# Four more pairs of adaLN vectors computed as rows on VectorE inside the SwiGLUs

## The chip, the cores and the metric

The kernel runs on one core of one Trainium2 chip. The metric is the device time of one execution in microseconds (us); all times here are in that unit unless a line says ns. The engines of the core are named as in the profile: PE is TensorE's matrix multiply and PEld its load of stationary operands, DVE is VectorE, ACT is ScalarE, POOL is GpSimd, SP is the engine that issues most of the transfers.

## What is computed

Two layers of a diffusion backbone: 256 latent and 256 context tokens of width 1024, in fp32. A layer is a SwiGLU, four token mixers that share one normed input, and a second SwiGLU. Before each of the three stands an RMS norm that is modulated by a shift and a scale, and behind each a gate; the nine vectors (three times shift, scale, gate) are the adaLN vectors, made from a conditioning vector, one set for the latent and one for the context tokens:

```python
mod  = (silu(c)     @ ada_w[l] + ada_b[l]).reshape(B, 1, N_ADA, D_MODEL)   # latent
modc = (silu(c_ctx) @ ada_w[l] + ada_b[l]).reshape(N_ADA, D_MODEL)         # context
sh1, sc1, g1, sh2, sc2, g2, sh3, sc3, g3 = [mod[:, :, i] for i in range(N_ADA)]
x = x + 0.5 * g1 * swiglu(modulate(rms_norm(x, norm_g[l, 0]), sh1, sc1), w_gate, w_up, w_down)
y, yc = token_mixers(modulate(rms_norm(x, norm_g[l, 1]), sh2, sc2), ...)
x = x + g2 * y
x = x + 0.5 * g3 * swiglu(modulate(rms_norm(x, norm_g[l, 2]), sh3, sc3), ...)
# the same for the context tokens; at the end rms_norm(x, final_g)

def rms_norm(x, g):      return x * rsqrt(mean(x * x) + RMS_EPS) * g
def modulate(x, shift, scale):  return x * (1.0 + scale) + shift
def swiglu(x, w_gate, w_up, w_down):
    return (silu(x @ w_gate) * (x @ w_up)) @ w_down     # inner width 2816 = 22 * 128
```

What the change touches is only how `mod` and `modc` are computed; a vector has 1024 values for each of the two conditionings.

## The kernel before

**Layout.** Activations lie with the channels on the partitions: `x[m]`, m = 0 to 7, is a tile of 128 channels by 512 tokens (256 in the last SwiGLU, which has only the latent tokens). Every product of the network is made in three parts from operands that are split into a high part `h` and a low part `l` (`mm3`: h by h, h by l, l by h). So each weight tile `wr` is cast by ScalarE into `wh` (L315) and VectorE makes `wl` as the difference (L316), in two halves of 512 columns. While the last SwiGLU of layer 0 runs, the weights of layer 1 that are called LOWS (36 parts) are split ahead: `low_part` loads 0.52 MB, splits it and stores 1.05 MB to DRAM.

**A SwiGLU** is `ffn`. It goes through three groups of inner tiles, GROUPS: 8, 8 and 6. In a group there is first an *up step* for each inner tile (products `gu` of gate and up, 48 in all, then tanh and the multiplications), then eight *down sums* m = 0 to 7 (products `dn`: 24 in a group of 8, 18 in a group of 6), each of which ends with a residual `resid` on VectorE (L660), which adds the gated sum to `x[m]`, one instruction for latent and one for context tokens. Behind every up step and every down sum `side` is called: it may emit one step of side work, so that this stands between the instructions of the SwiGLU.

**A norm** is `norm` with `stats`: ScalarE squares the eight `x` tiles (the first into `nacc`, L505, the others into `sq`, L508), GpSimd adds six of the squares to `nacc` (L510), TensorE sums over channels with a product by ones, first of `nacc`, then of the eighth square (both are called `st`), VectorE takes ten small steps for the inverse root (`rsqrt`, L366 to L376), TensorE transposes the result to all partitions (`B`, L356). Then, per tile, VectorE forms `xg` (L543), ScalarE adds the shift into `uh` (L545) and VectorE makes the low part `ul` (L546); the next `gu` or mixer products use `uh` and `ul`.

**adaLN vectors** are computed in nine pairs per layer, PAIRS; a pair is named by (layer, index), and the index of a gate's pair is 2 (first SwiGLU), 5 (mixer) and 8 (second SwiGLU). There are two ways:

- `ada(l, i)` on TensorE: eight loads `aw` of 0.52 MB, sixteen fp32 products `ada` (32 records in the profile), then a copy by ScalarE, four transposes `adaT` and a few small VectorE steps.
- `ada_rows(l, i)` on VectorE: eight steps, each with one load `aw` of 0.52 MB, two multiplications with a running sum, `aj` (L472, one for each conditioning, 128 by 1024), and an addition of the bias (L475). VPAIRS lists the pairs that go this way; the weights for them are laid out transposed on the host.

Rows are side work of `ffn`. Before, `side` emits one step of rows after each up step, and after a down sum only where no LOWS are left; it emits one `low_part` after every step of either kind while there are any. The SwiGLUs had as rows: first of layer 0 and first of layer 1 the pairs 3, 4, 6, 7; second of layer 0 the pairs (1,0) and (1,1), and the LOWS. The gates' pairs are done by `ada` at the borders: (0,5) and (1,5) behind the norm ahead of a mixer, (0,8) and (1,8) behind the norm ahead of the second SwiGLU, (1,2) between the layers' SwiGLUs.

**What sets the order.** The kernel is written in program order, and a scheduler fixes one static order for each engine from it, by priorities and from its own estimate of when operands and buffers are ready. Buffers rotate: 3 for a raw weight `wr`, 8 each for `wh` and `wl`, 6 for the small tiles (`sq`, `nacc`, `xg`, `aj` and others), 5 or 6 for `aw`. A load can start when the buffer's earlier user is done; loads are issued in order on SP's queue.

The borders, in order of time: 439 us, first SwiGLU of layer 0 to its mixer; 1150 us, that mixer to the second SwiGLU; 1526 us, second SwiGLU to the first of layer 1; 1896 us, that SwiGLU to the mixer of layer 1; 2349 us, that mixer to the last SwiGLU.

## Time and profile before

| | before |
|---|---|
| three runs, us | 2561.84, 2573.04, 2575.85 |
| median, us | 2573.04 |
| the profiled execution, us | 2568.95 |
| its span, first to last instruction, us | 2567.2 |
| PE busy | 2491.3 us, 97% |
| DVE busy | 1714.1 us, 67% |
| ACT busy | 1080.1 us, 42% |
| POOL busy | 146.9 us, 6% |
| transfers | 444.56 MB, mean 173 GB/s |
| granted TensorE clock, mean | 0.989 |
| share of PE in the chain that ended last | 53% |

The profile page is one execution, taken by the hardware profiler. A busy time is the union of an engine's instructions; the granted clock is 1.00 at 2.4 GHz and 0.50 at 1.2 GHz. In a timeline, rows of the same kind that follow each other are folded into one with xN, its time being the busy time of all of them. What stands in brackets is the idle time of the engine ahead of the row and the engine, tile and line that ended it. A product written `128*32 128x512` has a stationary operand of 128 by 32 and a moving one of 128 by 512.

### The profile page before, as it was taken

The numbers are of one execution on the slowest core, as the hardware profiler recorded it, in microseconds if no ns is written. First come the engines' busy times: TensorE is split into PE (matmuls) and PEld (weight loads), VectorE is DVE, ScalarE is ACT, GpSimd is POOL, SyncE is SP. The second block draws the span as 40 slices with busy tenths as digits, with TensorE's granted clock in tenths as the row PEclk, the third lists the DMA queues.
The fourth block names the chain that finished last, engine by engine and source line by source line (L and its number), as shares of the span: only waits on it lengthen the run. The fifth ranks groups of instructions, "written<-read, shape, count | busy, mean of one in ns | idle before, by whom it ended". The sixth has DMA issues, their size and how long they took to land.

```text
span 2567.2 us, 37223 instructions
## 1 busy us (share of the span) xinstructions
PE 2491.3 (97%) x13624; PEld 2055.4 (80%) x13624; DVE 1714.1 (67%) x3533; ACT 1080.1 (42%) x2127; POOL 146.9 (6%) x212
## 2 busy tenths in 40 slices
PE   7999999999999999999999999999999999899998
PEld 4778887898877767777888878888888778797998
DVE  5667767677556768747676557767457666676665
ACT  4433223433555564434444433232345653254554
POOL 0110001000000000010000010000010034300000
PEclk9999999999999999999999999999999999999999
DMA  7455546332413123238998944545244379755554
GB/s 256 168 196 196 173 145 205 119 116 90 141 56 125 62 74 111 93 116 286 325 333 320 326 146 148 181 136 194 85 166 167 105 212 269 217 177 206 181 181 124
DMA packets 163847, 444.56 MB, mean 173 GB/s; under 512 B 18698, under 2 KB 24268, under 8 KB 163664
## 3 DMA queue, kind: packets, MB, share of 16 engines
q1 hardware_dynamic: 142928, 404.42, 46.8%
q0 software_dynamic: 20736, 37.76, 5.3%
q8 instruction: 108, 1.77, 0.3%
q14 instruction: 75, 0.61, 0.1%
HBM read 383.91 MB, written 58.20 MB: 172 GB/s over the span
## 4 chain that ended last, share of the span: by engine, by line
PE 53%; DVE 3%; DMA 2%; issue 1%; ACT 1%; POOL 0%; DVEq 0%; POOLq 0%; ACTq 0%
PE gu L305 24%; PE dn L305 12%; PE gate L305 6%; PE wo L305 3%; PE tm L305 2%; PE ada L305 1%; PE dp L305 1%; PE br L305 1%; PE O L305 1%; PE S L305 1%; PE PT L356 1%; PE Og L305 0%; DVE wl L316 0%; DMA wh<-h_w_gate 0%; PE bk L305 0%
## 5 line engine op out<-in xcount | busy, mean ns | idle before, releaser
L315 ACT CAST wh<-wr 128x512 fp32r<-128x512 f32 (+1 forms) x854 | 517.1, 613 | 945.0 <-PE gu L305 335.0
L316 DVE TENSOR_TENSOR wl<-wr,wh 128x512 fp32r<-128x512 f32 (+1 forms) x854 | 572.6, 680 | 351.1 <-ACT wh L315 341.0
L305 PE MATMUL gu<-uh,wh 128*128 128x512 f32 (+1 forms) x1408 | 512.1, 366 | 3.6 <-ACT uh L545 2.8
L305 PE MATMUL gu<-ul,wh 128*128 128x512 f32 (+1 forms) x1408 | 512.1, 365 | 0.0
L305 PE MATMUL gu<-uh,wl 128*128 128x512 f32 (+1 forms) x1408 | 511.7, 364 | 0.1
L305 PE MATMUL dn<-hh,wh 128*128 128x512 f32 (+1 forms) x1408 | 390.1, 363 | 0.0
L305 PEld LDWEIGHTS gu<-uh,wh 128*128 128x128 f32 x1408 | 265.6, 189 | 54.4 <-ACT uh L545 10.1
L305 PEld LDWEIGHTS gu<-uh,wl 128*128 128x128 f32 x1408 | 265.3, 188 | 50.0 <-issue 6.7
L305 PEld LDWEIGHTS gu<-ul,wh 128*128 128x128 f32 x1408 | 265.7, 189 | 46.0 <-issue 2.5
L305 PEld LDWEIGHTS dn<-hh,wh 128*128 128x128 f32 x1408 | 253.0, 188 | 41.2
L305 PE MATMUL dn<-hh,wl 128*128 128x512 f32 (+1 forms) x704 | 255.8, 363 | 0.0
L305 PE MATMUL gate<-uh,wh 128*128 128x256 f32 (+1 forms) x768 | 199.9, 325 | 6.5 <-DMA wh<-h_w_gate 5.4
L472 DVE SCALAR_TENSOR_TENSOR aj<-aw,crow 128x1024 bf16<-128x1024 f32 x160 | 194.1, 1223 | 0.0
L305 PE MATMUL gate<-uh,wl 128*128 128x512 f32 (+1 forms) x512 | 176.1, 344 | 0.4 <-DMA wl<-l_w_gate 0.4
L305 PEld LDWEIGHTS dn<-hh,wl 128*128 128x128 f32 x704 | 132.6, 188 | 20.8
L510 POOL TENSOR_TENSOR nacc<-nacc,sq 128x512 f32<-128x512 f32 (+1 forms) x39 | 45.9, 1176 | 1800.7 <-ACT sq L508 1791.9
L305 PEld LDWEIGHTS gate<-uh,wh 128*128 128x128 f32 x768 | 130.0, 193 | 18.5 <-DMA wh<-h_w_gate 5.8
L305 PE MATMUL tm<-wh,uh 128*128 128x256 f32 x576 | 139.3, 287 | 0.4 <-ACT uh L545 0.4
L305 PE MATMUL tm<-wl,uh 128*128 128x256 f32 x432 | 123.1, 285 | 0.0
L660 DVE SCALAR_TENSOR_TENSOR x<-dn,gt,x 128x256 f32<-128x256 f32 x168 | 74.4, 478 | 57.9 <-PE dn L305 57.9
L305 PE MATMUL tm<-wh,ul 128*128 128x256 f32 x416 | 108.7, 287 | 0.0
L305 PEld LDWEIGHTS gate<-uh,wl 128*128 128x128 f32 x512 | 98.2, 192 | 12.6 <-issue 1.9
(416 smaller groups left out, 3918.8 us busy)
## 6 DMA issues: line engine op xcount, KB each, us to landing
wr<-in_gu SPq DMA_DIRECT2D x176, 512.0 KB, 4.3
aw<-in_adat SPq DMA_DIRECT2D x80, 512.0 KB, 3.6
wr<-in_dn SPq DMA_DIRECT2D x64, 512.0 KB, 4.1
aw<-in_ada SPq DMA_DIRECT2D x48, 512.0 KB, 4.9
wr<-in_w_gate SPq DMA_DIRECT2D x48, 512.0 KB, 3.5
wr<-in_w_tm SPq DMA_DIRECT2D x36, 512.0 KB, 4.2
wr<-in_dn SPq DMA_DIRECT2D x32, 384.0 KB, 3.2
wr<-in_w_br SPq DMA_DIRECT2D x24, 512.0 KB, 3.5
```

The lines of the kernel that those rows point to most:

```text
L305: self.nc.tensor.matmul(out, l, r, start=start, stop=stop)
L315: self.nc.scalar.copy(h, src)
L316: (eng or self.nc.vector).tensor_sub(l, src, h)
L356: self.nc.tensor.transpose(out, src, self.ident[:p, :p])
L472: nc.vector.scalar_tensor_tensor(out=x, in0=w, scalar=1.0, in1=self.crow[s], op0=ALU.mult, op1=ALU.mult, accum_out=o[:, s:s + 1])
L510: (nc.vector if first and k % 2 else nc.gpsimd).tensor_add(acc[:, :n], acc[:, :n], sq[:, :n])
L660: self.nc.vector.scalar_tensor_tensor(out=self.x[m][:, c], in0=p[:, c], scalar=gt[:, m, s:s + 1], in1=self.x[m][:, c], op0=ALU.mult, op1=A ...
```

## The change

Four pairs go over from `ada` to `ada_rows`: (0,5), (0,8), (1,2) and (1,8). VPAIRS grows from 10 to 14 pairs; the calls of `ada` for these pairs are taken out, and the pairs are given to `ffn` as rows: (0,5) to the first SwiGLU of layer 0 (five pairs instead of four), (1,2) and (1,8) to the first SwiGLU of layer 1 (six instead of four), (0,8) to the second SwiGLU of layer 0 (three instead of two). The pair (1,5) stays on TensorE.

`side` is written anew. It counts the row steps still to do and the steps of the SwiGLU that are left. After an up step it emits one row, or two where more rows are to do than steps are left for them; after a down sum it emits a row where no LOWS are left. The LOWS go behind the down sums; behind an up step one goes only while more LOWS are left than down sums.

```diff
--- before.py
+++ after.py
@@ -27,7 +27,7 @@
 
 PAIRS = ((0, 2), (1, 3), (4, 5), (6, 8), (7, 9), (10, 11), (12, 14), (13, 15), (16, 17))
 
-VPAIRS = ((0, 3), (0, 4), (0, 6), (0, 7), (1, 0), (1, 1), (1, 3), (1, 4), (1, 6), (1, 7))
+VPAIRS = tuple((l, i) for l in range(DEPTH) for i in range(9) if (l, i) not in ((0, 0), (0, 1), (0, 2), (1, 5)))
 GROUPS = ((0, 8), (8, 16), (16, 22))
 
 
@@ -591,14 +591,21 @@
     def ffn(self, l, f, u, n, gt, filler=(), rows=(), lows=()):
         nc, A = self.nc, self.A
         filler = list(filler)
-        rows, lows = self.rows(rows), list(lows)
-
-        def side(low_only=False):
+
+        todo, rows, lows = 8 * len(rows), self.rows(rows), list(lows)
+        left = {True: KF, False: KD * len(GROUPS)}
+
+        def side(up):
+            nonlocal todo
+            left[up] -= 1
             if filler:
                 filler.pop(0)()
-            elif not (low_only and lows):
-                next(rows, 0)
-            if lows:
+            elif up or not lows:
+                room = left[True] + (0 if lows else left[False])
+                for _ in range(2 if up and todo > room + 1 else 1):
+                    next(rows, 0)
+                    todo -= 1
+            if lows and (not up or len(lows) > left[False]):
                 self.low_part(lows.pop(0))
 
         for g0, g1 in GROUPS:
@@ -622,7 +629,7 @@
                 h, lo = self.pair("fh", "hh", n, "fl")
                 self.two(h[:, :n], lo[:, :n], t[:, :n])
                 hs.append((h, lo))
-                side()
+                side(True)
             if gt.__class__ is tuple:
                 gt = self.gate(*gt)
             q = g1 - g0
@@ -633,7 +640,7 @@
                     self.mm3(p[:, :n], w(j * P, P), (hs[j][0][:, :n], hs[j][1][:, :n]),
                              j == 0, j == q - 1)
                 self.resid(p, m, n, gt)
-                side(True)
+                side(False)
         for _ in rows:
             pass
 
@@ -1412,16 +1419,14 @@
             if l == 0:
                 step = lambda: next(f, 0)
                 fill = [step, step, step, lambda: self.ada(0, 2)] + [step] * 6 + [self.spread]
-            else:
-                self.ada(l, 2)
-            self.ffn(l, 0, u, NT, (l, 0, 0.25), fill, later(l, 3, 4, 6, 7))
+            self.ffn(l, 0, u, NT, (l, 0, 0.25), fill, later(l, 2, 3, 4, 6, 7, 8) if l else later(l, 3, 4, 5, 6, 7))
             u = self.norm(*self.gain(l, 1), NT, self.xd[l], last)
-            self.ada(l, 5)
+            if last:
+                self.ada(l, 5)
             self.mixer(l, u, last)
             self.phase("ffn")
             u = self.norm(*self.gain(l, 2), n)
-            self.ada(l, 8)
-            self.ffn(l, 1, u, n, (l, 2, 0.25), (), [] if last else later(l + 1, 0, 1), () if last else LOWS)
+            self.ffn(l, 1, u, n, (l, 2, 0.25), (), [] if last else later(l, 8) + later(l + 1, 0, 1), () if last else LOWS)
             if not last:
                 u = self.norm(*self.gain(l + 1, 0), NT)
         self.norm(self.v["final_g"], None, L)
```

Lines below the change move by 5 to 7: the residual's L660 is L667 in the kernel after.

The scheduler's order moves with it. First ScalarE at the border of 439 us: `wh` are the casts of the next weights (those of the mixer among them), `sq` and `nacc` the squares of the residuals `x_130` to `x_144` (m = 0 to 7). Before:

```order
L315 CAST wh_3845<-wr_3843 128x512
L315 CAST wh_3849<-wr_3843 128x512
L508 ACTIVATE sq_3662<-x_138 128x512
L315 CAST wh_3895<-wr_3893 128x512
L315 CAST wh_3899<-wr_3893 128x512
L508 ACTIVATE sq_3666<-x_140 128x512
L315 CAST wh_3954<-wr_3952 128x512
L315 CAST wh_3958<-wr_3952 128x512
L508 ACTIVATE sq_3670<-x_142 128x512
L315 CAST wh_3991<-wr_3989 128x512
L315 CAST wh_3995<-wr_3989 128x512
L508 ACTIVATE sq_3674<-x_144 128x512
```

After:

```order
L315 CAST wh_3906<-wr_3904 128x512
L315 CAST wh_3910<-wr_3904 128x512
L505 ACTIVATE nacc_3701<-x_130 128x512
L508 ACTIVATE sq_3706<-x_132 128x512
L508 ACTIVATE sq_3710<-x_134 128x512
L508 ACTIVATE sq_3714<-x_136 128x512
L508 ACTIVATE sq_3718<-x_138 128x512
L508 ACTIVATE sq_3722<-x_140 128x512
L508 ACTIVATE sq_3726<-x_142 128x512
L315 CAST wh_3965<-wr_3963 128x512
L315 CAST wh_3969<-wr_3963 128x512
L508 ACTIVATE sq_3730<-x_144 128x512
```

The squares, which alternated with the casts, stand in one run behind the casts of the mixer's second weight tile; the eighth comes behind one more pair of casts. At the border of 1896 us they stand in the same way.

VectorE at the same border, from the residual of m = 5 to the first step of the inverse root; `wl` are the low parts of the same weights, `aj` the rows. Before:

```order
L660 SCALAR_TENSOR_TENSOR x_140<-dn_3560,gt_1364,x_140 128x256 x2
L316 TENSOR_TENSOR wl_3900<-wr_3893,wh_3899 128x512
L316 TENSOR_TENSOR wl_3955<-wr_3952,wh_3954 128x512
L660 SCALAR_TENSOR_TENSOR x_142<-dn_3591,gt_1364,x_142 128x256 x2
L316 TENSOR_TENSOR wl_3959<-wr_3952,wh_3958 128x512
L316 TENSOR_TENSOR wl_3992<-wr_3989,wh_3991 128x512
L660 SCALAR_TENSOR_TENSOR x_144<-dn_3622,gt_1364,x_144 128x256 x2
L316 TENSOR_TENSOR wl_3996<-wr_3989,wh_3995 128x512
```

After:

```order
L472 SCALAR_TENSOR_TENSOR aj_3694,mod0_229<-aw_3692,crow_1631 128x1024
L472 SCALAR_TENSOR_TENSOR aj_3696,mod0_229<-aw_3692,crow_1633 128x1024
L316 TENSOR_TENSOR wl_3857<-wr_3854,wh_3856 128x512
L475 TENSOR_TENSOR mod0_229<-mod0_229,vec_98 128x2
L667 SCALAR_TENSOR_TENSOR x_142<-dn_3633,gt_1364,x_142 128x256 x2
L316 TENSOR_TENSOR wl_3861<-wr_3854,wh_3860 128x512
L316 TENSOR_TENSOR wl_3907<-wr_3904,wh_3906 128x512
L316 TENSOR_TENSOR wl_3911<-wr_3904,wh_3910 128x512
L316 TENSOR_TENSOR wl_3966<-wr_3963,wh_3965 128x512
L316 TENSOR_TENSOR wl_3970<-wr_3963,wh_3969 128x512
L484 SCALAR_TENSOR_TENSOR G_10700<-mod0_229,vec_98 128x16
L667 SCALAR_TENSOR_TENSOR x_144<-dn_3671,gt_1364,x_144 128x256 x2
```

After, the residual of m = 5 (`x_140`) stands right ahead of the first row shown. A last row step now stands behind the residual of m = 5, six `wl` and the step that forms `G` stand around that of m = 6, and none between the eighth and the inverse root; two more `wl` stand between the small steps of the inverse root.

Then ScalarE at the border of 1526 us; `lwh` are the casts of a `low_part`, `wh` those of weights. Before:

```order
L315 CAST wh_14282<-wr_14280 128x512
L315 CAST wh_14286<-wr_14280 128x512
L508 ACTIVATE sq_14124<-x_10367 128x512
L315 CAST wh_14317<-wr_14315 128x512
L315 CAST wh_14321<-wr_14315 128x512
L508 ACTIVATE sq_14127<-x_10369 128x512
L315 CAST wh_14371<-wr_14369 128x512
L315 CAST wh_14375<-wr_14369 128x512
L508 ACTIVATE sq_14130<-x_10371 128x512
L315 CAST wh_14406<-wr_14404 128x512
L315 CAST wh_14410<-wr_14404 128x512
L508 ACTIVATE sq_14133<-x_10373 128x512
```

After:

```order
L315 CAST wh_14091<-wr_14085 128x256
L315 CAST lwh_14120<-lw_14116 128x512
L315 CAST lwh_14126<-lw_14116 128x512
L505 ACTIVATE nacc_14134<-x_10370 128x512
L508 ACTIVATE sq_14137<-x_10372 128x512
L508 ACTIVATE sq_14140<-x_10374 128x512
L508 ACTIVATE sq_14143<-x_10376 128x512
L508 ACTIVATE sq_14146<-x_10378 128x512
L508 ACTIVATE sq_14149<-x_10380 128x512
L508 ACTIVATE sq_14152<-x_10382 128x512
L508 ACTIVATE sq_14155<-x_10384 128x512
L315 CAST wh_14259<-wr_14257 128x512
```

The squares, which alternated with the casts of the coming weights, now stand in one run behind the casts of the last `low_part`.

## Rows read from the trace of the kernel before

**Rows 1.** The page, part 1: busy time, share, instructions of each engine

```profile
PE 2491.3 (97%) x13624; PEld 2055.4 (80%) x13624; DVE 1714.1 (67%) x3533; ACT 1080.1 (42%) x2127; POOL 146.9 (6%) x212
```

**Rows 2.** Timeline, border B: start, us, engine line operation out<-in xcount, idle before

```profile
1155.42 1.92 PE L305 MATMUL ada<-aw,cs 128*32 128x512 f32 x4
1155.61 1.26 DVE L543 SCALAR_TENSOR_TENSOR xg<-x,G,B 128x256 f32<-128x256 f32 x3 [1.29 <-PE B L356]
...
1163.57 0.40 PE L305 MATMUL gu<-ul,wh 128*128 128x512 f32 x1
1163.90 1.05 PE L305 MATMUL ada<-aw,cs 128*32 128x512 f32 x4
1164.88 0.50 PE L305 MATMUL gu<-uh,wl 128*128 128x512 f32 x1
...
1175.24 0.60 PE L356 MATMUL adaT<-ident,adaev 128*128 128x128 f32 x4
```

**Rows 3.** Timeline of TensorE, border D

```profile
2353.88 1.92 PE L305 MATMUL ada<-aw,cs 128*32 128x512 f32 x4 [1.07 <-DMA aw<-in_ada]
2355.73 1.22 PE L305 MATMUL gu<-uh,wh 128*128 128x256 f32 x4
```

**Rows 4.** Timeline, border A

```profile
438.53 0.39 PE L305 MATMUL dn<-hh,wl 128*128 128x512 f32 x1
...
440.50 0.86 DVE L660 SCALAR_TENSOR_TENSOR x<-dn,gt,x 128x256 f32<-128x256 f32 x2
...
443.43 1.87 PE L305 MATMUL st<-ones,sq 128*128 128x1 f32 x8
...
446.91 0.16 DVE L376 SCALAR_TENSOR_TENSOR rs<-rs_a,rs_z 128x4 f32<-128x4 f32 x1
...
448.79 0.80 PE L356 MATMUL B<-ident,rs 128*128 128x128 f32 x4
```

**Rows 5.** Timeline of VectorE, last down sums before border A

```profile
410.87 0.87 DVE L660 SCALAR_TENSOR_TENSOR x<-dn,gt,x 128x256 f32<-128x256 f32 x2
...
414.96 0.87 DVE L660 SCALAR_TENSOR_TENSOR x<-dn,gt,x 128x256 f32<-128x256 f32 x2
...
419.35 1.22 DVE L472 SCALAR_TENSOR_TENSOR aj<-aw,crow 128x1024 bf16<-128x1024 f32 x1
420.49 2.30 DVE L472 SCALAR_TENSOR_TENSOR aj<-aw,crow 128x1024 bf16<-128x1024 f32 x1
```

**Rows 6.** Timeline of GpSimd, ahead of borders A and E

```profile
420.25 3.70 POOL L510 TENSOR_TENSOR nacc<-nacc,sq 128x512 f32<-128x512 f32 x2 [249.84 <-ACT sq L508]
...
1890.10 1.29 POOL L510 TENSOR_TENSOR nacc<-nacc,sq 128x512 f32<-128x512 f32 x1 [2.79 <-ACT sq L508]
```

**Rows 7.** Timelines of TensorE and of VectorE, border E

```profile
1896.38 0.95 PE L305 MATMUL st<-ones,nacc 128*128 128x1 f32 x8
1896.58 0.88 DVE L660 SCALAR_TENSOR_TENSOR x<-dn,gt,x 128x256 f32<-128x256 f32 x2 [0.20 <-PE dn L305]
1899.09 1.05 PE L305 MATMUL st<-ones,sq 128*128 128x1 f32 x8
```

**Rows 8.** Timeline of TensorE, border C

```profile
1526.14 0.95 PE L305 MATMUL st<-ones,nacc 128*128 128x1 f32 x8
...
1528.86 1.05 PE L305 MATMUL st<-ones,sq 128*128 128x1 f32 x8
...
1533.98 0.73 PE L305 MATMUL gu<-uh,wh 128*128 128x512 f32 x2 [0.61 <-ACT uh L545]
```

**Rows 9.** Windows: stretch, length, busy PE PEld DVE ACT POOL, PEclk, DMA share, GB/s

```profile
1530.00:1531.00 1.00, 1.00 (x9) 0.22 (x2) 0.83 (x6) 0.00 (x0) 0.00 (x0) 1.00 0.93 381
1153.00:1154.00 1.00, 0.00 (x0) 0.00 (x0) 0.86 (x7) 0.00 (x0) 0.00 (x0) 0.50 1.12 356
1384.00:1428.00 44.00, 44.00 (x196) 36.42 (x194) 26.08 (x48) 16.73 (x29) 0.00 (x0) 1.00 0.93 329
1493.00:1526.00 33.00, 33.00 (x147) 27.31 (x147) 16.36 (x32) 13.92 (x24) 7.73 (x6) 1.00 0.37 113
```

## The prediction

> **What bounds the kernel now.** I read the busy times first: TensorE is busy 97% of the span, VectorE 67%, GpSimd 6% [rows 1]. So time is to be had only where TensorE waits or does work that could go elsewhere, and it waits at the borders between a SwiGLU and a norm. I then read the timeline at each border the change touches. There are five: A (first SwiGLU of layer 0 to its mixer, 439 us), B (mixer of layer 0 to its second SwiGLU, 1150 us), C (that SwiGLU to layer 1, 1526 us), E (first SwiGLU of layer 1 to its mixer, 1896 us) and D (mixer of layer 1 to the last SwiGLU, 2349 us). A, B, C, D each lose a pair of products. At all of them the chain is the same: last residual on VectorE, its square on ScalarE, the two sums `st`, the rsqrt steps on VectorE, the transposes `B`, the first normed tile. A pair that lies inside this chain's idle time costs nothing; one that stands among `gu` products costs its full time.
>
> **What the removed products cost.** A pair is 32 records of `ada` in eight groups of four, and four transposes.
> B: after a `gu` at 1163.57 the next one would issue 0.23 later (a down sum of 18 products takes 4.08 to 4.09, so 0.227 each [rows 5]); with a group between, it issued at 1164.88 [rows 2]. That is 1.08 per group. Seven groups stand so: 7.6. The first lies in the wait for the normed tile (1155.42 for 1.92, while the first xg starts at 1155.61 and the tile takes about 1 us): about 0.5. The transposes at 1175.24 cost about 0.4 [rows 2]. I take 8.3, bounds 6.5 and 8.5.
> D: the first group waited 1.07 for its DMA and then ran 1.92 at the lower clock, so the first `gu` came at 2355.73 [rows 3]; its input should stand ready at about 2354, so 1.8. Seven groups by the same 1.08 and the transposes: 8.0. Together 9.8; I take 9.2 because here the sums are half as wide and the normed tiles may come late; bounds 7 and 9.8.
> C: 20 of the 32 records fill the idle time round `st`, the third group runs before the first normed tile; two groups are in the stream, 2.1, and the transposes 0.4: 2.5.
> A: nearly all lies in idle time, but some of it in the chain's way. The transposes `B` started at 448.79 though rs started at 446.91 and lasted 0.16: held 1.65 by fourteen records. Transposes of the pair 0.3. So 1.95.
> Sum of what goes: 8.3 + 9.2 + 2.5 + 1.95 = 22.
>
> **What the added rows cost.** Four pairs are 64 `aj` instructions of 1.22 [rows 5], 78 us of VectorE, inside stretches where TensorE sets the pace, so in the middle of a SwiGLU they cost nothing: an up step lasts 10.9 us (48 products), of which even two rows (four aj, 4.9) leave VectorE 6, and in the last group's down sums it keeps TensorE's pace exactly with two aj in each (residuals at 410.87 and 414.96, 4.09 apart [rows 5]). Their 32 loads of 0.52 MB take the place of the 32 removed; they leave the borders, where a pair's first group waited for one [rows 3], for stretches with room on the queue of SP, so I cost them at nothing. That exactness is the trouble. Before, the rows ended four sums before border A and a whole group before E. Now they run into the last sums of both, where GpSimd adds the squares for the norm. One aj beside these adds took 2.30 instead of 1.22 [rows 5], while two adds took 3.70 [rows 6] where one alone takes 1.29. So an add pushes VectorE back by 1.1, and VectorE has no slack to take it back.
> The scheduled order sharpens this. On ScalarE the squares no longer alternate with the casts of the next weights; seven of them stand behind the casts of the mixer's second weights, which need buffers that the sixth down sum gives back. So all six adds start some 6 us before the last down sum ends and meet a VectorE that still has an aj, six wl and two residuals to do. Six adds by 1.1 is 6.6; with about half a microsecond of slack in the last two sums, the last residual comes about 6 us after its sum.
> A: it came 2.0 after its sum (438.53 plus 0.39, then 440.50); at about 444.9 now, and `st` follows 1.65 later (0.87, a square of 0.63 and two hand-overs): 446.6 for 443.43 [rows 4], 3.2 later. Two wl now stand between the rsqrt steps: 1.2. With 1.95 off: **A +2.5**, bounds -3 (adds that never meet an aj) and +6.
> E: the last residual came 0.2 after its sum (1896.38, 1896.58); now at about 1902.4, `st` ready at 1904.0 for 1899.09 [rows 7]: 4.9. The two wl: 1.2. The pair (1, 5) stays on TensorE with five of its sixteen products between the two halves of `st`; they can now start only after the last add: 1.9 more. TensorE stands idle for over 4 us and should fall to 1.2 GHz, as it did in the wait at B (granted 0.50 at 1153 [rows 9]): 1. **E +9**, bounds +2.7 and +12.
> The Trainium skill (SBUF — State Buffer, "SBUF: two separate sides") says that a VectorE instruction with two SBUF inputs and a GpSimd instruction that reads SBUF exclude each other for a whole instruction, and that one with a single SBUF input is left alone. The 2.30 agrees. By it the residuals, which read PSUM, would slip past an add: A and E would each come 1.3 us earlier, and the sum below would be -1.6 instead of 1.0.
> C is another case. The copies of layer 1's weights (`low_part`: 0.52 MB read, 1.05 MB written) are moved from the up steps to the down steps, so eight of them now fall into the last eight down sums, and all squares stand on ScalarE behind the last copy's casts. Those sums need 8 x (1.57 + 0.39) = 15.7 MB in 33 us; a stretch full of copies moved 329 GB/s [rows 9], or 10.9 MB. About 5 MB can be loaded ahead (five row buffers, seven weights) and the last 1 MB written later, so the last cast comes about 4 us before the last sum ends: 9.7 MB by 329 GB/s is 29 us. Two squares and six adds of 1.29 later `st` can run: 5 us after the sum, and 6.7 with some waiting for VectorE, where it ran 2.7 after (1526.14, 1528.86 [rows 8]): 4. Three wl in the rsqrt steps and before the first xg: 1.8. The wl of the seventh sum's weights stand behind the residual of the sixth: a stall of 1.2. Only one and a half weights are ready at the border where four were: 1.5, a guess bounded by 0 and 4. And the clock: the pair kept TensorE busy from 1526 to the first `gu` at 1533.98, granted 1.00 at 1530; without it the clock falls as at B, to 0.50, that is 1.2 of 2.4 GHz [rows 8, 9]: 1. With 2.5 off: **C +7.0**, bounds 0 and +15.
>
> **The sum.** A 2.5, B -8.3, C 7.0, D -9.2, E 9.0: +1.0 us. The profiled execution took 2568.95 (span 2567.2 and 1.75 around it), so 2570; it lies 4 us under the median of the three runs, 2573.04, by which it would be 2574. I take the middle: 2572, no change. A measurement of this kernel can tell about 0.5%, 13 us, from no change.
>
> **Rivals.**
> 1. The borders don't get longer. If the adds find VectorE free and the copies keep up, A, C and E stand at their lower bounds, -3, 0 and +2.7, and with B and D the sum is -18: 2553, faster. For it: a single stretched aj is all that the rows show. Against: the order puts the adds where VectorE has no gap.
> 2. The copies at C outrun the DMA engines: slower than before. ScalarE and VectorE keep their order, so when a copy's store is late, the wl of the next sum's weights behind it is late, and TensorE waits inside the down sums. It decides once less than about 2 MB was loaded ahead: with 1 MB, 13.7 MB by 329 GB/s is 42 us, 9 past the sum's end, so the squares start 13 later than I took: C +20 and the sum +14, 2585, and with E at its upper bound +17: 2588. For it: the stretch before already stood at a DMA share of 0.93 with fewer bytes per us. Against: the load falls in the up steps ahead (0.37 in the last sums before [rows 9]).
> 3. The change doesn't free TensorE: at B and D the `gu` products then wait for the normed tiles, so nothing is won. VectorE makes a tile pair in 1.7 (four of the xg and ul, 1.26 for three [rows 2]), TensorE uses twelve products of 0.227 on it, 2.7, so B isn't limited so. If both gave half, the sum is +10: 2581, not told from no change.
>
> **How the numbers follow.** Forecast 0.58 (its own range 2560 to 2583), rival 1 0.20, rival 2 0.16, rival 3 0.06. Only rival 1 is faster by over 0.5%: 0.20. Rival 2 is slower by about 0.5%, and so are the upper bounds of C and E together within the forecast: 0.18. The rest, 0.62, lies within. The range reaches to both rivals and leaves out about a tenth on either side: 2553 to 2590.
>
> **What would show it.** Right: no `ada` at 440, 1155, 1527 and 2354; `gu` products without a gap there, so that the stretches from the border to the first full-rate `gu` are 8 to 9 us shorter at B and D. At A and E aj of 2 us beside the adds, the last residual 5 to 7 us after its down sum, TensorE idle there 10 us and at the lower clock. At C squares in one run after the last copy, the last add well past the last product. Wrong: residuals within 2 us of their sums at A and E (rival 1), or TensorE waiting for wl inside the last down sums before C (rival 2), or waits for uh and ul in `gu` at B and D (rival 3).

## The result, and the profile after

The changed kernel takes 2580.86 us (median of 20 runs, 2573.85 to 2585.94) where the kernel before, over 20 runs, takes 2565.84 (2559.73 to 2576.38). The ratio is 1.0056, 95% interval 1.0047 to 1.0065: it is slower by 15 us. The 2572 of the forecast stood for "no change" against a median of three runs that lay 7 us above the median of twenty; as a difference, I forecast +1.0, no change, and the change costs +15. The time lies in the range; that it would be slower was not forecast.

The busy times of the changed kernel, the answer to [rows 1], then its waits of TensorE (engine, line and tile that waited, what it waited for: us in all, times, longest):

```profile
PE 2476.0 (96%) x13480; PEld 2063.8 (80%) x13480; DVE 1789.6 (69%) x3677; ACT 1075.8 (42%) x2123; POOL 147.7 (6%) x212
```

```profile
PE st L305 <- POOL nacc L510: 30.1, 4, 14.6
PE B L356 <- DVE rs L376: 11.2, 5, 2.8
PE gu L305 <- ACT uh L545: 6.6, 4, 2.2
...
PE gu L305 <- DVE wl L316: 4.3, 2, 2.2
...
PE dn L305 <- ACT wh L315: 2.2, 1, 2.2
```

The same view of the kernel before:

```profile
PE st L305 <- POOL nacc L510: 14.7, 2, 13.6
PE B L356 <- DVE rs L376: 5.6, 3, 1.9
...
PE gu L305 <- ACT uh L545: 2.8, 2, 2.2
```

TensorE does 144 records less (four pairs, 32 records and four transposes each) and is busy 15 us less, but it waits 31 us more in these five lines: 15.4 for GpSimd's sums of squares, 5.6 for the inverse root, 3.8 for normed tiles, 4.3 and 2.2 for weights. The three kinds of wait at the top are at the borders; the last two are new, and stand inside the SwiGLUs.

Where the 16 us arise is read from landmarks, instructions that both kernels have, in both timelines (`st` of TensorE at the end of a SwiGLU or mixer, and ScalarE's first instruction on a finished gate product, `ft`, one for each up step):

| landmark | before | after | difference |
|---|---|---|---|
| ft, last up step ahead of A | 401.02 | 401.53 | +0.5 |
| st, end of the mixer, B | 1149.57 | 1152.77 | +3.2 |
| ft, third up step behind B | 1194.56 | 1190.71 | -3.85 |
| ft, fourth up step behind B | 1206.37 | 1206.32 | -0.05 |
| ft, last up step ahead of C | 1488.40 | 1488.88 | +0.5 |
| st, C | 1526.14 | 1535.21 | +9.1 |
| ft, first up step behind C | 1549.16 | 1556.42 | +7.3 |
| ft, fourth up step behind C | 1575.97 | 1589.42 | +13.45 |
| ft, last up step ahead of E | 1858.64 | 1872.08 | +13.4 |
| st, E | 1896.38 | 1915.60 | +19.2 |
| st, end of the mixer, D | 2348.70 | 2373.73 | +25.0 |
| ft, third up step behind D | 2380.18 | 2396.46 | +16.3 |

From one to the next this gives, against the prediction: A with its mixer +2.7 (predicted +2.5); B -7.0 at the border (-8.3), but +4.3 in the steps behind it (nothing); C +13.0 (+7.0); E with its mixer +11.6 (+9); D -8.7 (-9.2).

Each of these is taken from one profiled execution of each kernel and holds its chances. The kernel after and the run with short additions (below) have the same order to the instruction, and nothing that differs ahead of A's last sums, yet the second is 4.7 earlier at the first landmark: behind waits of TensorE of 0.7, 2.1 and 1.1 at 48, 82 and 172 us the granted clock was 0.50 in the first and 1.00 in the second, whose waits were as long. So a difference of 2 us or less between the stages of two executions says little by itself.

**Borders A and E.** VectorE's timeline ahead of A (answers to [rows 4, 5]) and, last, GpSimd's:

```profile
434.40 1.77 DVE L316 TENSOR_TENSOR wl<-wr,wh 128x512 fp32r<-128x512 f32 x1
436.10 1.25 DVE L475 TENSOR_TENSOR mod<-mod,vec 128x2 f32<-128x2 f32 x1
437.27 0.86 DVE L667 SCALAR_TENSOR_TENSOR x<-dn,gt,x 128x256 f32<-128x256 f32 x2
438.05 6.81 DVE L316 TENSOR_TENSOR wl<-wr,wh 128x512 fp32r<-128x512 f32 x5
...
444.87 0.86 DVE L667 SCALAR_TENSOR_TENSOR x<-dn,gt,x 128x256 f32<-128x256 f32 x2
```

```profile
434.19 9.52 POOL L510 TENSOR_TENSOR nacc<-nacc,sq 128x512 f32<-128x512 f32 x6 [262.75 <-ACT sq L508]
```

While GpSimd adds six squares, a `wl` takes 1.77 instead of 0.68, an addition of 128 by 2 takes 1.25 instead of 0.15, five `wl` take 6.81 (3.35 in the run with short additions, below); the two residual instructions between them take their usual 0.86. The additions are held back too: beside a `wl` one takes 1.6, alone 1.29. No `aj` meets them, at A or at E (the last one at A started at 433.26, before the additions, and took its 1.22), so the `aj` of 2 us that the prediction named as a sign did not come: `wl` and short instructions were held up in its place. The last residual comes 5.4 us behind the last sum, which ended at 439.44. The Trainium skill (SBUF — State Buffer, "SBUF: two separate sides"), weighed in the prediction, says that an instruction with two SBUF inputs and a GpSimd instruction that reads SBUF shut each other out for a whole instruction, and that one with a single SBUF input passes. The rows agree in both halves. TensorE at A, then at E (for [rows 4, 7]):

```profile
443.76 1.87 PE L305 MATMUL st<-ones,nacc 128*128 128x1 f32 x8 [4.33 <-POOL nacc L510]
446.51 1.87 PE L305 MATMUL st<-ones,sq 128*128 128x1 f32 x8 [0.88 <-ACT sq L508]
451.16 1.11 PE L356 MATMUL B<-ident,rs 128*128 128x128 f32 x4 [2.79 <-DVE rs L376]
453.47 0.58 PE L305 MATMUL tm<-wh,uh 128*128 128x256 f32 x1 [1.19 <-ACT uh L545]
...
1915.60 1.86 PE L305 MATMUL st<-ones,nacc 128*128 128x1 f32 x8 [5.62 <-POOL nacc L510]
1917.40 3.62 PE L305 MATMUL ada<-aw,cs 128*32 128x512 f32 x10
1920.95 1.87 PE L305 MATMUL st<-ones,sq 128*128 128x1 f32 x8
```

At both, the first wait is ended by GpSimd's last addition (at A the eighth square, behind the late residual, makes TensorE wait another 0.88), and TensorE then works at half the clock: eight `st` in 1.87 instead of 0.95 to 1.05, ten `ada` in 3.62 (1.90 in a run without this wait, below).

**Borders B and D.** TensorE at both (for [rows 2, 3]):

```profile
1160.62 2.07 PE L305 MATMUL gu<-uh,wh 128*128 128x512 f32 x4 [1.59 <-ACT uh L545]
1162.50 0.63 PE L305 MATMUL gu<-ul,wh 128*128 128x512 f32 x1
...
1199.38 0.73 PE L305 MATMUL gu<-uh,wl 128*128 128x512 f32 x1 [2.17 <-DVE wl L316]
...
2379.29 1.22 PE L305 MATMUL gu<-uh,wh 128*128 128x256 f32 x4 [1.19 <-ACT uh L545]
```

No `ada` stands between the `gu` any more, but the first ones come after a wait and at half the clock (the next starts 0.42 behind the one at 1162.50, not 0.23), and in the third up step behind B TensorE waits 2.17 for a low part of a weight.

**Border C and behind it.** TensorE's waits from the last down sums on:

```profile
1520.87 0.73 PE L305 MATMUL dn<-hh,wh 128*128 128x512 f32 x2 [2.25 <-ACT wh L315]
...
1535.21 1.87 PE L305 MATMUL st<-ones,nacc 128*128 128x1 f32 x8 [5.58 <-POOL nacc L510]
1541.58 1.11 PE L356 MATMUL B<-ident,rs 128*128 128x128 f32 x4 [2.79 <-DVE rs L376]
1544.28 1.22 PE L305 MATMUL gu<-uh,wh 128*128 128x512 f32 x2 [1.58 <-ACT uh L545]
...
1564.01 0.50 PE L305 MATMUL gu<-uh,wl 128*128 128x512 f32 x1 [2.10 <-DVE wl L316]
```

The first loads of layer 1's gate and up weights, on SP's queue, after and then before:

```profile
1527.10 0.32 SPq L662 DMA_DIRECT2D l_w_gate<-lwl  x1
1527.47 0.95 SPq L324 DMA_DIRECT2D wr<-in_gu  x2
```

```profile
1503.10 21.00 SPq L324 DMA_DIRECT2D wr<-in_gu  x6
```

Before, six weight tiles for the next layer were fetched between 1503 and 1524, under the down sums. After, they wait on the queue behind the last store of the last copy, and the first is asked for at 1527.5, two microseconds before the sums are over. The transfers in the last sums, for [rows 9], in the view of windows:

```profile
1494.00:1529.00 35.00, 32.76 (x143) 26.48 (x142) 20.38 (x41) 14.64 (x28) 1.81 (x2) 1.00 0.91 321
```

### The profile page after: what moved, and what is told of

It is laid out like the page before. It is cut to its first block, busy times and chain, and to the rows that moved or that the text cites. A ratio compares the mean times of both kernels' runs of the same rounds, so it can differ in the third digit from the quotient of the medians.

```text
span 2582.8 us, 37020 instructions
## 1 busy us (share of the span) xinstructions
PE 2476.0 (96%) x13480; PEld 2063.8 (80%) x13480; DVE 1789.6 (69%) x3677; ACT 1075.8 (42%) x2123; POOL 147.7 (6%) x212
## 3 DMA queue, kind: packets, MB, share of 16 engines
q8 instruction: 106, 1.74, 0.3%
## 5 line engine op out<-in xcount | busy, mean ns | idle before, releaser
L472 DVE SCALAR_TENSOR_TENSOR aj<-aw,crow 128x1024 bf16<-128x1024 f32 x224 | 269.8, 1217 | 2.5 <-DMA aw<-in_adat 1.7
L667 DVE SCALAR_TENSOR_TENSOR x<-dn,gt,x 128x256 f32<-128x256 f32 x168 | 74.4, 478 | 64.1 <-PE dn L305 64.0
```

The lines of the kernel that those rows point to most:

```text
L472: nc.vector.scalar_tensor_tensor(out=x, in0=w, scalar=1.0, in1=self.crow[s], op0=ALU.mult, op1=ALU.mult, accum_out=o[:, s:s + 1])
L667: self.nc.vector.scalar_tensor_tensor(out=self.x[m][:, c], in0=p[:, c], scalar=gt[:, m, s:s + 1], in1=self.x[m][:, c], op0=ALU.mult, op1=A ...
```

## The experiments

All ratios are to the kernel before on the same chip; the kernel after is 1.0056. In the stages named below, the border and the steps behind it are taken from the landmarks above.

### Two rows in the first up steps

In the second SwiGLU of layer 0 and the first of layer 1, the rule of `side` doubles exactly the first two up steps: there are two rows more to do than single steps.

```diff
-                for _ in range(2 if up and todo > room + 1 else 1):
+                for _ in range(2 if up and left[True] < KF - 3 and todo > room + 1 else 1):
```

> The kernel after, but no up step among the first three of a SwiGLU emits two rows; the doubled ones come later. Theory V (VectorE is full in the first two up steps behind a norm, where the normed tiles, two rows and the low parts of the weights meet): the waits of TensorE for wl of 2.2 us in the third up step behind border B and of 2.1 us in the second behind border C go, and with them the stretches at half the clock behind them; ahead of the first the kernel after stands 3.8 us ahead of before and behind it 0.5 us behind, at the second it falls from 7.3 to 13.5 us behind. So about 4 and 6 us: 10 us less than after, ratio to before 1.0017. Rival L (the waits come from the copies and rows that share the loads' queue, not from two rows): the stall behind border B stays, at most 2 us are won, ratio 1.005. Rival N (later doubles only shift the wait to a later up step): ratio 1.0056 as after.

Measured: 2572.98 us, ratio 1.0030 [1.0019, 1.0041]: 6.7 us less than after. Both waits for `wl` are gone. By the landmarks 1.2 us are won behind B, where waits of 0.73 and 0.21 for `wh` are new from the last sums of the same group on, and 4.0 at C; another 3.6 are won at E, where the order of rows and casts is that of the kernel after and only the half clock lasted 6.8 us and not 13.7. The second run leaves the loads where they are and takes away only VectorE's time, by leaving out most of the second rows' sums:

```diff
+                c = slice(0, 64 if self.thin else 1024)   # thin: second row of the first two up steps
-                nc.vector.scalar_tensor_tensor(out=x, in0=w, ..., in1=self.crow[s], ...)
+                nc.vector.scalar_tensor_tensor(out=x[:, c], in0=w[:, c], ..., in1=self.crow[s][:, c], ...)
```

> The kernel after, but the second row of each of the first two up steps in the second SwiGLU of layer 0 and the first of layer 1 multiplies only 64 of its 1024 columns: part of four adaLN values' sums is left out, the loads stay. Theory V (VectorE's time): eight multiplications of 1.22 become short ones, so 4.5 us of VectorE go in each of the two places; both waits for wl go, as in the run without early doubles: 8 to 10 us less than after, ratio 1.0017 to 1.0025. Rival L (the loads of two rows and a copy delay the weights' loads): loads are the same, the waits of 2.2 and 2.1 us stay, ratio 1.005 to 1.0056.

Measured: 2574.70 us, ratio 1.0031 [1.0020, 1.0042], the same gain. One wait for `wl` of 0.92 is left, a step later behind B; the one behind C is gone. By the landmarks 2.8 us are won behind B and 4.7 at C. So it is VectorE's time and not the loads: theory V, with less than its 8 to 10 us. VectorE has no pause there after C: the normed tiles keep it from 1542.8 to 1555.4, then rows and low parts follow, and the `wl` that TensorE waits for from 1561.9 on stands behind the fourth `aj`:

```profile
1562.12 1.22 DVE L472 SCALAR_TENSOR_TENSOR aj<-aw,crow 128x1024 bf16<-128x1024 f32 x1
...
1563.27 0.69 DVE L316 TENSOR_TENSOR wl<-wr,wh 128x512 fp32r<-128x512 f32 x1
```

The windows of the first steps behind B in the kernel after show VectorE full (10.23 and 11.00 of 11 us; the columns are those of [rows 9]):

```profile
1171.00:1182.00 11.00, 11.00 (x50) 9.10 (x49) 10.23 (x21) 6.12 (x12) 0.00 (x0) 1.00 0.19 57
1182.00:1193.00 11.00, 11.00 (x51) 9.09 (x49) 11.00 (x24) 5.18 (x9) 0.00 (x0) 1.00 0.88 281
```

### Rows that end earlier

```diff
-            elif up or not lows:
-                room = left[True] + (0 if lows else left[False])
+            elif up or not lows and left[False] >= KD:
+                room = left[True] + (0 if lows else max(left[False] - KD, 0))
```

> The kernel after, but rows end ahead of the last group's down sums, so that no multiplication of a row meets GpSimd's additions of squares; more up steps are doubled instead. In its order the squares alternate with the casts again at the borders of 439 and 1896 us. Theory R (rows in the last sums hold up the last residual and the additions): at border A the two st wait no longer for the last addition by 4.3 us, at E not by 5.6 us; E falls from +11.3 to about +4 and A from +2.5 to about 0, and the rsqrt steps lose the two wl: 8 to 10 us less than after, ratio 1.0018 to 1.0025. Rival K (the missing products of ada, whose idle time lets the clock fall to half, cost the time at A; E had its products all along): A stays at +2 to +3, E gains 5 at most: ratio 1.0035 to 1.004.

Measured: 2562.54 us, ratio 0.9983 [0.9972, 0.9995]: 18.7 us less than after, twice what theory R gave. By the landmarks A went from +2.7 to -4.1 and E from +11.6 to -0.9; B, C and D stayed (-7.6 and +4.2, +13.1, -9.1). VectorE and TensorE at E in this run:

```profile
1901.65 0.88 DVE L667 SCALAR_TENSOR_TENSOR x<-dn,gt,x 128x256 f32<-128x256 f32 x2 [0.20 <-PE dn L305]
```

```profile
1901.45 0.95 PE L305 MATMUL st<-ones,nacc 128*128 128x1 f32 x8
1902.33 1.90 PE L305 MATMUL ada<-aw,cs 128*32 128x512 f32 x10
1904.16 1.05 PE L305 MATMUL st<-ones,sq 128*128 128x1 f32 x8
```

The residual comes 0.20 behind its sum, as before the change, `st` waits for nothing, and the pair that stays there runs at the full clock. In the kernel after no `aj` stood beside the additions, so it is not quite what the expectation names that went: without rows in the last sums the squares alternate with the casts again, and each addition takes 1.29, 4.1 us behind the one before. What theory R had left out of the price of the wait is the second half of it: all that TensorE does behind it at half the clock.

Does the hold-up come from GpSimd's additions, or simply from the order, with `aj` and six `wl` ahead of the last residuals? One run keeps the order of after to the instruction and makes the additions short:

```diff
+                c = n if first else 64
-                (nc.vector if first and k % 2 else nc.gpsimd).tensor_add(acc[:, :n], acc[:, :n], sq[:, :n])
+                (nc.vector if first and k % 2 else nc.gpsimd).tensor_add(acc[:, :c], acc[:, :c], sq[:, :c])
```

> The kernel after in its own order, but GpSimd's additions of squares cover 64 of 512 columns in all norms but the first; the rest of these sums is left out. Theory G (a wl or aj of VectorE that runs beside such an addition is held up by it): at border A VectorE lost 1.1 on a wl, 1.1 on an addition of a bias and 3.8 on five wl while GpSimd added for 9.5 us; without that the last residual comes within 1 us of its sum at A and E instead of 5.4, and st 1.7 later. A and E fall by 4 to 5 each; at C, where VectorE is free and GpSimd's 8.0 us alone hold st, by 4: 13 us less than after, ratio 1.0005. Rival O (the order itself: rows and six wl ahead of the last residuals are too much for VectorE): the residuals stay 3 us or more behind, only C gains: ratio 1.003 to 1.004.

Measured: 2559.08 us, ratio 0.9976 [0.9964, 0.9988]: 20.5 us less than after. VectorE ahead of A, with rows, order and casts as in the kernel after:

```profile
430.72 0.88 DVE L668 SCALAR_TENSOR_TENSOR x<-dn,gt,x 128x256 f32<-128x256 f32 x2
431.51 3.35 DVE L316 TENSOR_TENSOR wl<-wr,wh 128x512 fp32r<-128x512 f32 x5
434.79 0.16 DVE L484 SCALAR_TENSOR_TENSOR G<-mod,vec 128x16 f32<-128x16 f32 x1
434.87 0.86 DVE L668 SCALAR_TENSOR_TENSOR x<-dn,gt,x 128x256 f32<-128x256 f32 x2
```

The five `wl` take 3.35 and not 6.81, the last residual starts 0.1 behind the end of its sum, and A stands at -3.7, E at -0.7, C at +5.4 instead of +13.0. That is more than theory G's 13 us: at E, which fell by 12.3, there is no stretch at half the clock either. Rival O is out: the order alone costs little, it is harmful through the additions, which it brings late and beside VectorE's tightest stretch. The run makes the additions short as well as harmless, so it doesn't tell how much of A and E is VectorE's hold-up and how much the additions' own 9.5 to 9.7 us. At C, where VectorE has little to do, it is the 8 us of the additions themselves that `st` waits for, since the squares start late there.

### The copies of layer 1's weights

```diff
-            if lows and (not up or len(lows) > left[False]):
+            if lows:
```

> The kernel after, but the 36 copies of layer 1's weights stand as in the kernel before, one behind every step of either kind until they are used up, so that none is left in the last down sums ahead of border C. Theory C (the copies in the last sums hold the squares and the next weights): st at border C comes 2.7 us behind its sum again and not 6, the wait for a weight cast of 2.2 us in the last sums goes, about 7 to 8 us less than after (the wait for wl in the second up step behind C, 2.1 us and the clock behind it, stays): ratio 1.0026 to 1.003. Rival F (the removed pair ada(1,2) is what lengthens C, since TensorE is idle and at half the clock there): less than 3 us won: ratio 1.0045 to 1.0056. Behind border B the first steps hold two rows and a copy as in the kernel after, so nothing changes there.

Measured: 2567.98 us, ratio 1.0004 [0.9994, 1.0013]: 13.3 us less than after, more than theory C's 7 to 8. C went from +13.0 to -1.4. The wait for `wl` in the second up step behind C went too, though that step still holds two rows, so the theory was wrong there: that wait needs both causes, a VectorE without room and weights that came too late to be split ahead. Behind B nothing changed (+4.2).

The copies without any pair moved, in the kernel before:

```diff
-            elif not (low_only and lows):
-                next(rows, 0)
-            if lows:
+            elif up or not lows:
+                ...
+            if lows and (not up or len(lows) > left[False]):
```

> The kernel before with the new side steps alone: no pair is moved, but the copies of layer 1's weights go mostly behind the down sums. Theory C (the copies in the last eight sums are what lengthens border C): a wait for a weight cast of about 2 us in the last sums, st 5 to 6 us behind the last sum, so C +6 to +9, everything else as before: ratio 1.0025 to 1.0035. Rival F (it needs the missing pair ada(1,2)): C within 2 us of before, ratio 1.000 to 1.001.

Measured: 2583.24 us, ratio 1.0073 [1.0058, 1.0087], 17 us more than before and twice theory C. All of it is at C (+17.3; E +0.2):

```profile
1532.16 1.86 PE L305 MATMUL st<-ones,nacc 128*128 128x1 f32 x8 [6.27 <-POOL nacc L510]
...
1545.89 0.50 PE L305 MATMUL gu<-uh,wh 128*128 128x512 f32 x1 [3.24 <-ACT wh L315]
1549.18 0.79 PE L305 MATMUL gu<-uh,wh 128*128 128x512 f32 x1 [2.55 <-ACT wh L315]
```

The wait for the sums of squares, which I had, is 6.3; two waits for the next layer's weights, 5.8 together, come on top. Those two are this run's own, by SP's queue:

```profile
1524.57 13.38 SPq L293 DMA_DIRECT2D aw<-in_ada  x6
1538.00 0.90 SPq L324 DMA_DIRECT2D wr<-in_gu  x2
```

The next layer's weights stand here behind the loads of the pair (1,2) and are first asked for 12 us behind the last sum; in the kernel after, which has no such loads, it is 2 us ahead of its end. So the copies in the last sums cost 17 with that pair on TensorE. With the pair moved their price is read from the run with late doubles: C stands at +9.0 there, at +13.0 with the doubled rows as well, and at -0.7 with neither (below).

### Both edits, and what is left

> Two edits of earlier runs together: rows end ahead of the last group's down sums, and the copies stand one behind every step as in the kernel before. If the two act at different borders and add up (theory S), the stages taken from the two earlier profiles give A -4.2, B -2.8 (with the wait for wl in the third up step still there), C -1.4, E -0.9, D -9.1: 18 us less than before, ratio 0.993. If they share a cause (rival: the same waits counted twice), the gains of 18.5 and 13 us over the kernel after don't add: 2562, ratio 0.998.

Rows ended early and copies as before: 2551.29 us, ratio 0.9943 [0.9929, 0.9958], 14.6 us less than before (theory S: 18). The gains over after, 18.7 and 13.3, add up to 32; measured 29. They act at different borders, theory S.

Without doubled steps in the first group of a SwiGLU, on top of both:

```diff
-                for _ in range(2 if up and todo > room + 1 else 1):
+                for _ in range(2 if up and left[True] < KF - 8 and todo > room + 1 else 1):
```

> As the run with both edits, but no up step of the first group emits two rows; the doubled ones stand in the second and third group. Theory V (in the first up steps behind a norm VectorE has no room for a second row): the wait for wl of 2.2 us behind border B goes with its stretch at half the clock: 3 to 4 us less than the run with both, ratio 0.9915. Rival M (the work only moves: the run without early doubles won 5 us there and gave 3.4 back at the end of the same group, in waits for wh): at most 1 us, ratio 0.993.

Measured: 2548.11 us, ratio 0.9932 [0.9918, 0.9945]. The wait for `wl` in the third up step behind B, 1.73 with both edits, is gone, but two of 1.15 and 1.09 are new in the first up steps of the second group, where the doubled rows now stand, and by the landmarks the steps behind B win 0.7 in all: that is rival M. The two intervals overlap; that the time is lower by 3 us is not shown.

And TensorE kept busy while it waits at the four borders:

```diff
+    def warm(self, k):                       # k transposes that nothing uses
+        ps = self.pss("warm")
+        for i in range(k):
+            self.tr(ps[:, i % 4 * P:i % 4 * P + P], self.ident)
...
+            if warm:
+                self.warm(8 if last else 3)  # behind each of the two st; 6 more behind B
```

> As the run with both edits, but at borders A, B, C and D TensorE is given 17 transposes of the identity that nothing uses: 3 between the two st, 8 behind them, 6 behind B. They stand where it waits for the inverse root and the first normed tile. Theory H (without the products of a pair TensorE waits there and is granted half the clock, which then lasts 5 us into the next products: at B 11 gu at 0.427 us instead of 0.227, the transposes B at 1.11 instead of 0.65, the st at 1.46 instead of 0.95): 2.5 to 3.5 us at each of the four borders, so 10 us less than the run with both, ratio 0.989. Rival W (the clock falls all the same, or the transposes delay B and the first products): no gain, ratio 0.993 to 0.995.

Measured: 2547.82 us, ratio 0.9931 [0.9917, 0.9945], 3.5 below the run with both edits where theory H had 10. The scheduler placed them well only at B: of their 32 records there, 15 stand between the two `st`, 14 behind them and 3 behind `B`. The windows at B (the last number but two is the granted clock), first with both edits, then with the transposes:

```profile
1144.00:1148.00 4.00, 1.59 (x9) 1.10 (x8) 1.96 (x12) 0.00 (x0) 0.00 (x0) 0.54 0.95 356
1148.00:1152.00 4.00, 2.98 (x7) 2.40 (x8) 4.00 (x12) 2.62 (x6) 0.00 (x0) 0.50 1.02 411
```

```profile
1146.00:1150.00 4.00, 3.75 (x35) 3.49 (x33) 1.50 (x10) 0.00 (x0) 0.00 (x0) 1.00 0.90 348
1150.00:1154.00 4.00, 2.74 (x13) 2.11 (x12) 4.00 (x11) 2.43 (x6) 0.00 (x0) 1.00 1.01 400
```

TensorE stays at 2.4 GHz through the border, and by the landmarks B falls from -7.1 to -9.6: 2.5 us, the lower end of what theory H gave for a border. At C none stands in the wait, and C is the same in both runs (-0.7), at A and D the difference is 0.2. The intervals of the two runs overlap, but the next run bears it out. In the kernel before the clock had fallen at B too:

```profile
1152.40:1159.00 6.60, 4.77 (x13) 2.13 (x13) 4.89 (x19) 1.82 (x5) 0.00 (x0) 0.50 1.01 380
```

So the pair's products had not kept it up there, they had shortened the stretch at half the clock: 6.8 us with them, 10.2 in the kernel after.

> Rows end ahead of the last group's down sums, copies as in the kernel before, no doubled up step in the first group, and the 17 unused transposes at the four borders. The last two gained 3.2 and 3.5 us apart from each other (0.0011 and 0.0012 of before); behind border B they don't share a wait (one takes the wait for wl in the third up step, the other the half clock ahead of it). If they add up: 2545, ratio 0.992. If the clock's gain only moves TensorE earlier into a wait for wl (rival): ratio 0.993.

All together: 2545.75 us, ratio 0.9923 [0.9909, 0.9938], the lowest of all kernels here, 20 us below the kernel before and 34 below after. That is the 0.992 of the sum, though the interval holds the rival's 0.993 too. By the landmarks the transposes bring 2.2 us at B here and 3.9 with the steps behind it, and the same 3.9 between the two runs above.

> As the run without doubled up steps in the first group (ratio 0.9932), but only the pairs (0,8) and (1,8) are rows; (0,5) and (1,2) are products again at borders A and C. Theory P (at A and C a pair lies mostly in the norm's wait, but some of its products stand in the way): A loses the 4 us that the run with rows ended early had gained there, C about 1: ratio 0.9952. Rival Q (with the pair's products the clock stays up and the wait is filled, so the two pairs cost nothing there): ratio 0.9925 to 0.9932.

Only (0,8) and (1,8) as rows: 2550.23 us, ratio 0.9941 [0.9926, 0.9955], between the two theories. By the landmarks it is rival Q: A stands at -4.5 with the pair's products and at -4.9 without them, C at 0.0 and -0.7. By these stages (0,5) and (1,2), placed well, bring under a microsecond each; the times, 2 us apart with intervals that overlap, don't decide it. This run and the one with the copies alone also show that A's gain is not the pair's: with (0,5) on TensorE both have A 4 to 4.5 below the profiled execution of before. That one had its `st` wait 1.16 for GpSimd and then ran at half the clock ([rows 4]: eight `st` in 1.87); the others waited 0.42 or not at all and stayed at full clock. The wait in the kernel before:

```profile
440.08 1.05 PE L305 MATMUL st<-ones,nacc 128*128 128x1 f32 x8 [1.16 <-POOL nacc L510]
```

A differs by 4 us between executions with nearly the same order.

## Why the prediction was right or wrong

**What went was right.** B -7.0 for -8.3, D -8.7 for -9.2: the groups of `ada` among the `gu` products, 1.08 each, are worth what [rows 2, 3] say. The 1.3 lacking at B are no more than what half the clock costs there, since there are no products any more in the wait for the first normed tile: with that wait filled B stands at -9.6. Rival 3 is out: its sign, waits for `uh`, came only ahead of the first `gu` (1.59 and 1.19).

**A and E were right in kind and near in size.** The last residual was put 6 us behind its sum and came 5.4 (A) and 5.5 (E), `st` at A was put at 446.6 and came at 446.51; A gave +2.7 for +2.5, E +11.6 for +9. In this execution E's error is the clock term: I put 1 us on it, but twenty products of `ada`, both `st` and the first transposes run at half the clock. Three other runs with the same rows ahead of E had 6.8 us of half clock there in place of 13.7 and E at +8.0, +9.3 and +10.2, so the 2.6 lies mostly in the execution. The chain was not quite the one of the prediction: what `st` waited for first was the additions themselves, 9.5 and 9.7 us of them, and at E the late residual behind them held nothing. Rival 1 (borders that don't get longer) is out: A and E stand at +2.7 and +11.6, and additions that meet no `aj` cost as much. A's closeness is partly luck: the profiled execution of before had its own stretch at half the clock there, and against the runs with the pair on TensorE that had none, A would be +7. The 1.65 that I took off because `ada` held the transposes `B` came from the same stretch: those fourteen records took 3.63 there and 1.92 in the two other runs, where `B` started 0.1 behind the inverse root. What I did not see is that the rows need not meet the border at all: ended earlier, the same rows cost nothing there, and the two borders are 19 us better.

**The step that failed: "in the middle of a SwiGLU they cost nothing".** I took an up step of 10.9 us in the steady state, where two rows leave VectorE 6. But in the two SwiGLUs whose rows have to be doubled for two steps, `side` doubles the first two, and there VectorE also makes the 32 instructions of the normed tiles (12.6 us at C) and, behind B, a copy. Behind B the difference grew by 4.3, behind C by 6.2, 10.5 of the 15 us that the sum was off by. Not all of it is the rows': the two runs that take VectorE's second rows away from there are 6.4 to 6.7 us faster than after, and the 6.2 behind C needs the late weights as well (below). The row that would have told it is VectorE's occupation behind a border and not in an up step taken anywhere.

**C's border itself was right, its sequel not.** To the first `ft` behind C the difference grew by 6.8 where I had 7.0 for the whole of C. The squares came late as I said (5.6 us behind the sum, predicted 5 to 6.7, with a stall of 2.25 for 1.2 in the sums). The term that came out too small is "Only one and a half weights are ready at the border where four were: 1.5, a guess bounded by 0 and 4". SP's queue shows why: six loads of the next layer's weights, which ran under the sums before, stand behind the copies' stores. Together with the doubled rows these late weights cost the 6.2 of the second up step; with either cause taken away its wait for `wl` goes. Without the doubled rows (the run with late doubles) the difference grew by 1.4 from the first to the fourth `ft` behind C, near the 1.5 put down: the guess held for late weights alone, and not for both together. Rival 2 had the direction (copies that crowd the last sums, slower than before) and about the time, 2585, but not the place: TensorE lost 2.25 inside the sums where it had 9, and the rest behind the border.

So the sum failed mainly by terms I had put at nothing or guessed, not by those read from rows: start +0.5, A +0.2, B +1.3, behind B +4.3, C +6.0, E +2.6, D +0.5, together the 15.3 between +1.0 and +16.3, up to rounding.

## What to carry to other kernels

Work that is moved to an engine with idle time has to be looked at in the steps where it lands first: right behind a norm and in the last sums ahead of one, that engine is no longer idle, though its share of the whole span is 67%. A rule that spreads side work evenly should leave out these two stretches; with rows kept out of the last sums and the copies back in their old places, a loss of 14 us by the ratios became a gain of 15, and of 17 without doubled steps in the first group. And when loads or copies change places, the queue has to be read for what now stands behind them, since the next stage's first weights are the ones that pay.

## What the runs showed of the hardware

An addition on GpSimd of 128 by 512 holds up VectorE's instructions with two SBUF inputs whatever their size: an addition of 128 by 2 took 1.25 instead of 0.15, one of 128 by 16 at E 1.23 instead of 0.16, a `wl` of 128 by 512 1.74 to 1.77 instead of 0.68, while a residual with one input in PSUM kept its 0.47 (0.86 for the two). The additions themselves took 1.6 beside `wl` instead of 1.29. The loss of clock cost more than the waits ahead of it seem to: at A the granted clock was 0.50 from 442 to 459, though TensorE had products without a pause from 453.5 on, and with transposes of no use in the waits at B it was 1.00 and B 2.2 to 2.5 us shorter. And whether it falls is not fixed by the kernel: with the same order and the same waits it was 0.50 behind three waits of 0.7 to 2.1 us in one execution and 1.00 in another, 4.7 us apart.
